# Output projection of a decoder block: seven products of halves for the first half of its inner dimension

## The chip, the cores and the metric

The kernel runs on one core of one Trainium2 chip. The metric is the time of one execution in device microseconds (us); lower is better. A core has five engines with a queue of instructions each: TensorE (PE in the profile; its weight loads are PEld), VectorE (DVE), ScalarE (ACT), GpSimd (POOL) and SyncE (SP), which here only issues DMA transfers. Each queue is worked off in its order, and an instruction that waits holds up those behind it.

## The reference, cut to what matters

One decoder block on 512 tokens with 1024 channels: two branches (stick-breaking attention, an RWKV-7 time mix) are merged by gates, projected and added to the residual, then come a squared-ReLU MLP and gated per-layer embeddings. The change lies in the line with `w_out`, a product of 512 x 1024 by 1024 x 1024.

```python
    g_sb, g_rw = jnp.split(jax.nn.sigmoid(u_gate), 2, axis=-1)
    merged = g_sb * (o_sb @ w_up_sb[i]) + g_rw * (o_rw @ w_up_rw[i])
    x = x + merged @ w_out[i]
    h = rms_norm(x, mlp_norm_g[i])
    x = x + jnp.square(jax.nn.relu(h @ w_ff1[i])) @ w_ff2[i]
```

## The kernel before, in words

All matrix products of this part are made in three passes: each operand x is kept as a rounded part hi and a rest lo = x - hi, and a product is hi*hi + hi*lo + lo*hi. For a weight tile, ScalarE writes hi (`fetch_to`, L220) and VectorE writes lo (L221); for an operand `split` does the same (L266, L267). So a weight unit of 128 x 1024 numbers (512 KB) costs a DMA load (L178, into one of four buffers `w_raw`), an ACT cast and a DVE subtraction. The hi and lo tiles rotate through three buffers, except for units with a home of their own (`homes`).

The order of the weight units is written out by hand in the list `seq`. `weights` takes the next unit; three steps of matmuls later (`step`, L241 on) the two units behind it are cast and one more is loaded. The framework then orders each engine's queue by its own estimate of when instructions become ready, in which what stands earlier in the program goes first among the ready ones. So loads run ahead of their place in the program as far as buffers are free, and a queue's order on the chip may be one that its times do not suit.

The stage of the change runs as follows (L1117 on). First the residual input x (`xs`, four loads, L1122) and the embedding input (`praw`, L1124) are asked for. Then eight steps m = 0 to 7 make the merged activations: two tiles `ga` and `gb` are loaded (L1130, L1131), ScalarE applies a sigmoid to `gb` (L1133), TensorE makes the product of the RWKV branch for 128 channels (12 matmuls, lines 236 to 238), VectorE multiplies (L1141), adds (L1142), and `split` writes hi and lo into `mg` (128 channels x 512 tokens each; m is the index k of the inner dimension). Then comes the output projection, in `rows3` (lines 251 to 253): six matmuls of 512 columns multiply one group of 128 tokens (tt, four of them) with one weight unit. A unit of `w_out` holds 256 rows of the inner dimension (two k) by 512 columns; units 0 to 3 are the left half of the columns, 4 to 7 the right half. `by_token` makes the left half for all four groups of tokens, unit by unit. The right half is made group by group with all four units. `taken` (L1153, L1155) adds a result to `xs` and sums its squares; `scaled` (L1165 to L1169) makes the norm of a group of tokens once both halves are in. After the third group, `gained` transposes the first two groups into `hx` (L1092, L1096, L1097), the input of the MLP. Results take turns in the eight PSUM banks (`ps_main`: two of pool `psm`, six of pool `ps4`).

The MLP behind it already makes its second product of each quarter by seven products of halves. There the sums of weight blocks are made by DMAs that add onto a tile already in memory, issued on POOL's queue: in `early_sums` (L1338 to L1341) one tile is loaded and a block added onto it, and that tile is then added onto a second one; a third such place is L180.

## Time and profile before

| | us |
|---|---|
| median of 3 runs | 859.14 (859.08 to 859.78) |
| the profiled execution, its time | 859.45 |
| its span in the profile | 857.6 |
| PE busy in the span | 842.7 |
| DVE busy | 696.3 |
| ACT busy | 502.3 |
| POOL busy | 102.2 |

Busy time of PE is the time in which at least one matmul was under way; matmuls overlap, so the duration of one (389 ns for 512 columns) is more than the distance to the next. The other engines' instructions overlap only a little at their ends. A group's line gives its engine, its operation, the tile written and those read, the shapes, the count, the busy time and mean duration, and the idle time of the engine in front of it. A DMA's line in a queue is its issue; the time to landing is told apart.

### The profile page before, as it was taken

Reading aid. Unit: us, or ns where it says so; the run is one execution under the profiler, and the core shown is the slowest. Engines: PE = TensorE matmul, PEld = TensorE weight load, DVE = VectorE, ACT = ScalarE, POOL = GpSimd, SP = SyncE. Lnnn points to the kernel's source line nnn. Section 1 sums busy time; section 2 is a strip of 40 time slices with the busy share of each in tenths; the row PEclk is TensorE's granted clock in tenths of the full one; section 3 lists DMA queues with packets and bytes.
Section 4 is the critical chain, followed back from the end, with each engine's and each line's share of the span. In section 5 each row is a group of like instructions: output and inputs, shape, how many; then the busy total and the mean of one; then the engine's idle time right before and its main releaser. Section 6 shows DMA issues by size and latency. Waiting matters only on the chain.

```text
span 857.6 us, 14532 instructions
## 1 busy us (share of the span) xinstructions
PE 842.7 (98%) x5570; PEld 697.4 (81%) x5570; DVE 696.3 (81%) x1238; ACT 502.3 (59%) x785; POOL 102.2 (12%) x170
## 2 busy tenths in 40 slices
PE   9999999999999999999999999999999999999996
PEld 5778788877777777877888887899889989988885
DVE  7989987896987978867763489998789988997767
ACT  7788887744436253534554666467547844873843
POOL 1332431001202111020000101000110011010000
PEclk9999999999999999999999999999999999999998
DMA  8212212221121314428950766964875589284402
GB/s 321 99 51 64 84 62 86 75 99 51 63 88 37 109 66 136 162 86 275 328 183 25 212 205 152 246 192 134 210 223 150 149 226 260 83 225 136 173 24 99
DMA packets 39333, 121.08 MB, mean 141 GB/s; under 512 B 4448, under 2 KB 4448, under 8 KB 39264
## 3 DMA queue, kind: packets, MB, share of 16 engines
q1 hardware_dynamic: 34656, 103.37, 35.0%
q0 software_dynamic: 4608, 16.78, 11.0%
q8 instruction: 44, 0.72, 0.4%
q14 instruction: 25, 0.20, 0.1%
HBM read 105.46 MB, written 10.49 MB: 135 GB/s over the span
## 4 chain that ended last, share of the span: by engine, by line
PE 80%; DVE 13%; ACT 2%; DMA 2%; issue 2%; SPq 0%; DVEq 0%; ACTq 0%
PE ps_m L236 13%; PE ps_m L237 13%; PE ps_m L238 12%; PE ps_m L252 9%; PE ps_m L253 9%; PE ps_m L251 9%; DVE w_lo L221 2%; DMA w_raw<-in_wts_dram 2%; PE ps_g L862 1%; PE ps_o L542 1%; PE ps_s L990 1%; PE ps_z L550 1%; PE ps_g L952 1%; PE ps_c L981 1%; DVE LX L884 1%
## 5 line engine op out<-in xcount | busy, mean ns | idle before, releaser
L220 ACT CAST w_hi<-w_raw 128x1024 fp32r<-128x1024 f32 x123 | 129.0, 1050 | 133.0 <-PE ps_m L237 74.5
L221 DVE TENSOR_TENSOR w_lo<-w_raw,w_hi 128x1024 fp32r<-128x1024 f32 x123 | 150.3, 1224 | 32.0 <-ACT w_hi L220 31.5
L236 PE MATMUL ps_m<-h_hi,w_hi 128*128 128x512 f32 x320 | 130.2, 408 | 0.1
L238 PE MATMUL ps_m<-h_hi,w_lo 128*128 128x512 f32 x320 | 128.5, 402 | 0.0
L237 PE MATMUL ps_m<-h_lo,w_hi 128*128 128x512 f32 x320 | 128.1, 400 | 0.1
L238 PEld LDWEIGHTS ps_m<-h_hi,w_lo 128*128 128x128 f32 x320 | 60.2, 188 | 11.9
L236 PEld LDWEIGHTS ps_m<-h_hi,w_hi 128*128 128x128 f32 x320 | 60.6, 190 | 11.2 <-ACT h_hi L398 0.6
L237 PEld LDWEIGHTS ps_m<-h_lo,w_hi 128*128 128x128 f32 x320 | 60.4, 189 | 11.2 <-DVE h_lo L399 1.2
L237 PE MATMUL ps_m<-hx,w_hi 128*128 128x256 f32 (+1 forms) x212 | 68.6, 324 | 0.1
L236 PE MATMUL ps_m<-hx,w_hi 128*128 128x256 f32 (+1 forms) x212 | 68.6, 324 | 0.0
L238 PE MATMUL ps_m<-hx,w_lo 128*128 128x256 f32 (+1 forms) x212 | 68.5, 323 | 0.0
L252 PE MATMUL ps_m<-w_lo,fS 128*128 128x512 f32 x128 | 50.0, 391 | 0.6 <-DVE w_lo L221 0.6
L251 PE MATMUL ps_m<-w_hi,fS 128*128 128x512 f32 x128 | 49.8, 389 | 0.0
L236 PE MATMUL ps_m<-tb,w_hi 128*128 128x256 f32 x176 | 49.8, 283 | 0.0
L237 PE MATMUL ps_m<-tb,w_hi 128*128 128x256 f32 x176 | 49.8, 283 | 0.0
L238 PE MATMUL ps_m<-tb,w_lo 128*128 128x256 f32 x176 | 49.8, 283 | 0.0
L253 PE MATMUL ps_m<-w_hi,fS 128*128 128x512 f32 x128 | 49.8, 389 | 0.0
L237 PEld LDWEIGHTS ps_m<-hx,w_hi 128*128 128x128 f32 x212 | 40.4, 190 | 3.5 <-DVE hx L1097 0.4
L236 PEld LDWEIGHTS ps_m<-hx,w_hi 128*128 128x128 f32 x212 | 40.4, 190 | 3.4 <-ACT hx L1096 0.2
L238 PEld LDWEIGHTS ps_m<-hx,w_lo 128*128 128x128 f32 x212 | 40.3, 190 | 3.1
L251 PE MATMUL ps_m<-w_hi,fA 128*128 128x512 f32 x96 | 37.4, 389 | 0.0
L252 PE MATMUL ps_m<-w_lo,fA 128*128 128x512 f32 x96 | 37.4, 389 | 0.0
(410 smaller groups left out, 2107.4 us busy)
## 6 DMA issues: line engine op xcount, KB each, us to landing
w_raw<-in_wts_dram SPq DMA_DIRECT2D x130, 512.0 KB, 3.8
gates<-gg SPq DMA_DIRECT2D x16, 256.0 KB, 2.0
w_raw<-in_wts_dram POOLq DMA_DIRECT2D x8, 512.0 KB, 6.4
x_in<-in_xT_dram SPq DMA_DIRECT2D x8, 256.0 KB, 5.3
tmp<-gates SPq DMA_DIRECT2D x8, 256.0 KB, 3.2
upsb<-tmp SPq DMA_DIRECT2D x8, 256.0 KB, 3.9
ga<-upsb SPq DMA_DIRECT2D x8, 256.0 KB, 5.2
gb<-gates SPq DMA_DIRECT2D x8, 256.0 KB, 5.0
```

Of the source, the lines that this page charges most:

```text
L220: state["cast"] = act.copy(out=hi, in_=raw).ins
L221: dve.tensor_tensor(out=lo, in0=raw, in1=r32(hi), op=ALU.subtract)
L236: pe.matmul(ps, wh, xh[:, k, t], start=first, stop=False, skip_group_check=skip)
L237: pe.matmul(ps, wh, xl[:, k, t], start=False, stop=False, skip_group_check=skip)
L238: pe.matmul(ps, wl, xh[:, k, t], start=False, stop=last, skip_group_check=skip)
L251: pe.matmul(ps, xh[:, k + j], wh, start=first and j == 0, stop=False, skip_group_check=True)
L252: pe.matmul(ps, xh[:, k + j], wl, start=False, stop=False, skip_group_check=True)
L253: pe.matmul(ps, xl[:, k + j], wh, start=False, stop=last and j == 1, skip_group_check=True)
L542: pe.matmul(ps_o[:, j * P:T], vv[:, j, hh, :, :].rearrange("p a d -> p (a d)"), part[:, ZB[j]:ZB[j] + ZN[j]], start=j == 2 and part is wh, ...
L550: pe.matmul(zt[b][:, :n], tri, part[:, s:s + n], start=False, stop=False, skip_group_check=True)
L862: last = pe.matmul(ps[rows, k], left[rows, k, :], rhs[rows, k], start=True, stop=True)
L884: beside = dve.transpose(out=N[rows], in_=LM[rows, :, r // 2, r % 2 * 32:r % 2 * 32 + 32])
```

## The change

The four blocks of `w_out` that belong to the first half of the inner dimension (units 0, 1, 4, 5, called B11, B21, B12, B22) and the four blocks of the merged activations that meet them (A11, A12, A21, A22: tokens 0 to 255 or 256 to 511, by k = 0, 1 or k = 2, 3) are multiplied by seven products of blocks in place of eight (Strassen's scheme in Winograd's form). A product is two groups of tokens times one weight unit.

- `sums_by_dma`: three new tiles are loaded and summed by DMA: T3 = B12 + B22, T2 = B11 + T3, T4 = B21 + T2. Loads on SP's queue, additions on POOL's. A further sum, B11 + B12 for product 3, is made in a buffer `w_raw` by a load and an addition.
- `left_sums` and `lefts`: four sums of blocks of the activations, made by VectorE for k = 0, 2 (after m = 2) and k = 1, 3 (after m = 3), split into hi and lo, and kept in `hx`, which is free until then. The block A21 is not needed in itself, so for m = 0 and 1 only 256 tokens are split.
- `by_halves`: the products in the order 0, 3, 2, 1, 4, 5, 6 (the list `ORDER`), on eight PSUM banks: V, W, `seeded` and `rest`, two each. Product 0 goes to V, and ScalarE copies V to `seeded`; 3 goes to W, 2 is accumulated on V; ScalarE copies W and V aside; 1 is accumulated on `seeded`, 4 on V; VectorE subtracts what was set aside from W; 5 is accumulated on W; VectorE writes `rest`; 6 is accumulated on V. The weights are B11 for product 0, B21 for 1, T2 for 2, B11 + B12 for 3, T3 for 4, B22 for 5 and T4 for 6.
- The second half of the inner dimension (units 2, 3, 6, 7) is accumulated on the eight banks group by group, left and right half of the columns in turn; units 2, 3 and 6 have homes.
- `xs` and `praw` are asked for after the loop over m, `praw` is split after the seven products, `ga` and `gb` of more steps lie in buffers that are free early, and `sqx` has one buffer in place of two.

```diff
@@ -52,6 +52,8 @@
 SEVEN = {(1, kp) for kp in range(3)} | {(q, kp) for q in (2, 3) for kp in range(4)}
 EARLY = (0, 2)
 FF2_FROM = {0: 0, 1: 2, 3: 0, 5: 6}
+ORDER = (0, 3, 2, 1, 4, 5, 6)
+FROM = {0: 0, 1: 1, 3: 0, 5: 5}
 
 
 K_ID, K_ONE, K_STRICT, K_INCL, K_B8, K_O8, K_S8, K_BO8, K_BO, K_TRI, K_NEG, K_CAUS = range(12)
@@ -144,7 +146,7 @@
             [(U_GRW, m) for m in range(4, 8)] + [(U_UPSB, m) for m in range(4)]]
     seq += mixes(0) + sum(FILL, [])
     seq += [(U_UPRW, m) for m in range(4)]
-    seq += [(U_OUT, m) for m in range(8)]
+    seq += [(U_OUT, "s", i) for i in ORDER] + [(U_OUT, m) for m in (2, 3, 6, 7)]
     seq += [(U_PLE, 0)]
     for qd in range(4):
         for kp in range(4):
@@ -167,6 +169,8 @@
             return wts[UBASE[U_FF2] + seq[i][1] * 8 + FF2_FROM[seq[i][2]] + seq[i][3]]
         if seq[i][0] == U_S12:
             return wts[UBASE[U_FF1] + seq[i][1] * 8 + seq[i][2] + 4]
+        if seq[i][1] == "s":
+            return wts[UBASE[seq[i][0]] + FROM[seq[i][2]]]
         return wts[UBASE[seq[i][0]] + seq[i][1]]
 
     def load_to(n):
@@ -178,6 +182,8 @@
                 sync.dma_start(out=loaded[i], in_=unit(i))
                 if seq[i][0] == U_FF2 and seq[i][2] == 3:
                     pool.dma_start(out=loaded[i], in_=wts[UBASE[U_FF2] + seq[i][1] * 8 + 4 + seq[i][3]], accum_op=ALU.add)
+                if seq[i][1:] == ("s", 3):
+                    pool.dma_start(out=loaded[i], in_=wts[UBASE[seq[i][0]] + 4], accum_op=ALU.add)
 
     def four_sums(i):
 
@@ -337,7 +343,7 @@
                     todo.remove(t)
 
 
-        t12 = pa.tile([P, T], F32, name="t12")
+        t12 = pa.tile([P, T], F32, name="t12", tag="t12")
         t13 = pa.tile([P, T], F32, name="t13")
 
         def mixed(i, dst):
@@ -1082,6 +1088,59 @@
                 rows3(pss[tt], w, rhs, tt, kk * 2, kk == 0, kk == 3)
         return pss
 
+    def sums_by_dma(u, tile_):
+
+        t2, t3, t4 = (tile_(n) for n in ("T2", "T3", "T4"))
+        for t, m in ((t3, 4), (t2, 0), (t4, 1)):
+            sync.dma_start(out=t, in_=wts[UBASE[u] + m])
+        pool.dma_start(out=t3, in_=wts[UBASE[u] + 5], accum_op=ALU.add)
+        for t, more_ in ((t2, t3), (t4, t2)):
+            pool.dma_start(out=t, in_=more_, accum_op=ALU.add)
+        for i, t in ((2, t2), (4, t3), (6, t4)):
+            sources[u, "s", i] = lambda t=t: t
+
+    def by_halves(u, left, V, W, seeded, rest, spare):
+
+        def run(i, pss, first):
+            w = weights(u, "s", i)
+            for t2 in range(2):
+                rows3(pss[t2], w, left[i], t2, 0, first, False)
+
+        def aside(pss):
+            got = [spare() for _ in range(2)]
+            for t, ps in zip(got, pss):
+                act.copy(out=t, in_=ps)
+            return got
+
+        run(0, V, True)
+        for t2 in range(2):
+            act.copy(out=seeded[t2], in_=V[t2])
+        run(3, W, True)
+        run(2, V, False)
+        third, second = aside(W), aside(V)
+        run(1, seeded, False)
+        run(4, V, False)
+        for t2 in range(2):
+            dve.tensor_tensor(out=W[t2], in0=W[t2], in1=second[t2], op=ALU.subtract)
+        run(5, W, False)
+        for t2 in range(2):
+            dve.tensor_tensor(out=rest[t2], in0=third[t2], in1=V[t2], op=ALU.subtract)
+        run(6, V, False)
+        return (seeded + V, W + rest)
+
+    def left_sums(S, kp, a, b, c, d):
+
+        sums = const.tile([P, 4, 256], F32, name="sums", tag="lora_w")
+        for out_, x, y, op in ((0, d, b, ALU.subtract), (1, c, d, ALU.subtract), (2, sums[:, 0], c, ALU.subtract), (3, a, sums[:, 2], ALU.add)):
+            dve.tensor_tensor(out=sums[:, out_], in0=x, in1=y, op=op)
+        split(S[0][:, kp * 4:kp * 4 + 4], S[1][:, kp * 4:kp * 4 + 4], sums)
+
+    def lefts(x, S):
+
+        A11, A12, A22 = ([t[:, k:k + 2, h * 256:h * 256 + 256] for t in x] for k, h in ((0, 0), (2, 0), (2, 1)))
+        S1, S3, S2, S4 = ([t[:, i::4] for t in S] for i in range(4))
+        return (A11, A12, S2, S1, S3, S4, A22)
+
     def gained(gname, half, src):
 
         for kp in range(KT // 2):
@@ -1118,15 +1177,14 @@
     with ExitStack() as s3:
         p3 = s3.enter_context(tc.tile_pool(name="p3", bufs=1))
         mg = [pa.tile([P, KT, T], F32R, name="mg0", tag="h_lo"), p3.tile([P, KT, T], F32R, name="mg1")]
-        for tt in range(TT):
-            sync.dma_start(out=xs[:, tt, :], in_=xt[:, tt, :])
-        praw = p3.tile([P, 2, T], F32, name="praw")
-        sync.dma_start(out=praw, in_=pT)
+        S = [t[:, 0:4].rearrange("p a (b t) -> p (a b) t", b=2) for t in hx]
+        sums_by_dma(U_OUT, lambda n: p3.tile([P, 1024], F32, name=n))
+        ups = []
         for m in range(8):
 
-            early = {0: ("mix", "mix"), 1: ("mix", "mix"), 2: ("gg", "gg")}.get(m)
-            ga, gb = (pa.tile([P, T], F32, name=n, tag=early[j], bufs=4 if early[j] == "mix" else 2) if early else
-                      p3.tile([P, T], F32, name=n, bufs=3) for j, n in enumerate(("ga", "gb")))
+            ga = pa.tile([P, T], F32, name="ga", tag="mix", bufs=4) if m < 4 else p3.tile([P, T], F32, name="ga", bufs=2)
+            gb = pa.tile([P, T], F32, name="gb", tag="t12" if m % 3 == 2 else "gg", bufs=1 if m % 3 == 2 else 2)
+            ups.append(ga)
             sync.dma_start(out=ga, in_=upsb[:, m, :])
             sync.dma_start(out=gb, in_=gates[:, KT + m, :])
             with tc.issue_after(state["norm"].ins):
@@ -1140,18 +1198,25 @@
             product(ps, w, orw, nk=4, base=m % 2 * 512)
             dve.tensor_tensor(out=gb, in0=ps, in1=gb, op=ALU.mult)
             dve.tensor_tensor(out=ga, in0=ga, in1=gb, op=ALU.add)
-            split(mg[0][:, m, :], mg[1][:, m, :], ga)
-        split(pin[0], pin[1], praw)
+            n = 256 if m < 2 else T
+            split(mg[0][:, m, 0:n], mg[1][:, m, 0:n], ga[:, 0:n])
+            if m in (2, 3):
+                x, y = ups[m - 2], ga
+                left_sums(S, m - 2, y[:, 0:256], y[:, 256:T], x[:, 0:256], x[:, 256:T])
+        for tt in range(TT):
+            sync.dma_start(out=xs[:, tt, :], in_=xt[:, tt, :])
+        praw = p3.tile([P, 2, T], F32, name="praw")
+        sync.dma_start(out=praw, in_=pT)
         wo = [[p3.tile([P, 1024], F32R, name=f"wo{kk}{i}") for i in range(2)] for kk in range(3)]
-        for kk in range(3):
-            homes[(U_OUT, 4 + kk)] = lambda kk=kk: wo[kk]
+        for kk, m in enumerate((2, 3, 6)):
+            homes[(U_OUT, m)] = lambda kk=kk: wo[kk]
         xsc = pa.tile([P, TT, D], F32, name="xsc", tag="h_hi")
 
         def taken(ps, tt, half):
 
             xb = xs[:, tt, COLHALF[half]]
             dve.tensor_tensor(out=xb, in0=ps, in1=xb, op=ALU.add)
-            sq = p3.tile([P, T], F32, name="sqx", bufs=2)
+            sq = p3.tile([P, T], F32, name="sqx")
             act.activation(out=sq, in_=xb, func=AF.Square, accum_out=st2[:, half, tt:tt + 1])
             if half == 0:
                 a, ah = st2[:, 0, tt:tt + 1], st2[:, 2, tt:tt + 1]
@@ -1167,16 +1232,16 @@
             dve.tensor_scalar(out=vh, in0=b, scalar1=-0.5 / D, scalar2=ah, op0=ALU.mult, op1=ALU.add)
             newton(r, n, vh, dve)
             state["scaled"] = act.activation(out=xsc[:, tt], in_=xs[:, tt], func=AF.Copy, scale=r).ins
-        pss = by_token(U_OUT, 0, mg, 0)
+        V, W, seeded, rest = ([ps_main() for _ in range(2)] for _ in range(4))
+        pss = by_halves(U_OUT, lefts(mg, S), V, W, seeded, rest, lambda: pa.tile([P, T], F32, name="aside", tag="mix", bufs=4))
+        split(pin[0], pin[1], praw)
+        ws = [weights(U_OUT, m) for m in (2, 3, 6, 7)]
+
         for tt in range(TT):
-            taken(pss[tt], tt, 0)
-        ws = [weights(U_OUT, 4 + kk) for kk in range(4)]
-
-        for tt in range(TT):
-            ps = ps_main()
-            for kk in range(4):
-                rows3(ps, ws[kk], mg, tt, kk * 2, kk == 0, kk == 3)
-            taken(ps, tt, 1)
+            for half in range(2):
+                for kk in range(2):
+                    rows3(pss[half][tt], ws[half * 2 + kk], mg, tt, 4 + kk * 2, False, kk == 1)
+                taken(pss[half][tt], tt, half)
             scaled(tt)
             if tt == 2:
                 gained("mlp_g", 0, xsc)
```

## The prediction

> **What bounds the kernel now.** I read the page first, then the waits of PE, then the timeline of the output projection.
>
> ```profile
> span 857.6 us, 14532 instructions
> PE   842.7 (98%) x5570; PEld 697.4 (81%) x5570; DVE 696.3 (81%) x1238; ACT 502.3 (59%) x785; POOL 102.2 (12%) x170
> L220 ACT CAST w_hi<-w_raw 128x1024 fp32r<-128x1024 f32 x123 | 129.0, 1050 | 133.0 <-PE ps_m L237 74.5
> ```
>
> PE is busy almost always. Its longest waits in the whole execution are small:
>
> ```profile
> PE ps_z L381 <- POOL warm L378: 1.3, 1, 1.3
> ...
> PE ps_m L252 <- DVE w_lo L221: 0.6, 2, 0.4
> ```
>
> In the stage of the change PE never stops, so here a matmul saved is time saved, and any wait put in front of one is time lost. The timeline of PE shows the first matmul of the projection (L251), the transposes within it and the first matmul behind it (`pins`):
>
> ```profile
> 424.80 0.39 PE L251 MATMUL ps_m<-w_hi,mg 128*128 128x512 f32 x1
> ...
> 462.89 1.91 PE L1092 MATMUL ps_m<-cst,xsc 128*128 128x128 f32 x16
> 464.55 0.48 PE L251 MATMUL ps_m<-wo,mg 128*128 128x512 f32 x1
> ...
> 470.10 0.39 PE L251 MATMUL ps_m<-w_hi,pins 128*128 128x512 f32 x1
> ```
>
> From 424.80 to 470.10 are 45.30 us; the transposes take 464.55 - 462.89 = 1.66. The other 43.64 hold 8 units x 4 groups x 6 = 192 matmuls, one per 0.227 us (the 0.39 of a row is its length; the next starts inside it).
>
> **Matmuls.** The first half of the inner dimension had 96 of them. Seven products of two groups x 6 = 12 make 84, and the second half keeps 96. So 12 go: 12 x 0.227 = 2.7 us, all on the path. This is also the ceiling, because PE had no wait here that could vanish. Each product now lasts 2.72 us where a unit lasted 5.45; the products start at 424.80, 427.5, 430.2, 433.0, 435.7, 438.4 and 441.1, the second half at 443.9.
>
> **VectorE.** Its groups from 402 to 445 us now:
>
> ```profile
> L221 DVE TENSOR_TENSOR w_lo<-w_raw,w_hi 128x1024 fp32r<-128x1024 f32 x8 | 9.8, 1220 | 5.4 <-ACT w_hi L220 5.4
> L1142 DVE TENSOR_TENSOR ga<-ga,gb 128x512 f32<-128x512 f32 x8 | 5.4, 686 | 0.1
> L267 DVE TENSOR_TENSOR mg<-ga,mg 128x512 fp32r<-128x512 f32 x8 | 5.4, 684 | 1.5 <-DMA upsb<-tmp 0.8 <-ACT mg L266 0.7
> L1141 DVE TENSOR_TENSOR gb<-ps_m,gb 128x512 f32<-128x512 f32 x8 | 5.4, 682 | 0.6 <-PE ps_m L238 0.6
> L221 DVE TENSOR_TENSOR wo<-w_raw,wo 128x1024 fp32r<-128x1024 f32 x3 | 3.6, 1212 | 0.0
> ...
> L267 DVE TENSOR_TENSOR pins<-praw,pins 128x1024 fp32r<-128x1024 f32 x1 | 1.2, 1225 | 2.9 <-ACT pins L266 2.9
> ```
>
> These are 30.8 us in 43. The added work has its like in the MLP, where the same sums and copies are made:
>
> ```profile
> L267 DVE TENSOR_TENSOR fS<-sums,fS 128x1024 fp32r<-128x1024 f32 x7 | 8.5, 1221 | 2.3 <-ACT fS L266 2.2
> L1217 DVE TENSOR_TENSOR sums<-sums,rr 128x256 f32<-128x256 f32 x7 | 3.0, 424 | 0.2
> ...
> L1191 ACT COPY rr<-ps_m 128x512 f32<-128x512 f32 x3 | 1.6, 595 | 0.0
> ...
> L1365 DVE TENSOR_TENSOR xs<-xs,ps_m x56: 678/680/684, 529.5 to 797.1; 128x512 f32<-128x512 f32 x56
> ```
>
> Three more weight units (11 for 8) are 3 x 1.22 = 3.7; `left_sums` 2 x (4 x 0.42 + 1.22) = 5.8; four subtractions from PSUM 4 x 0.68 = 2.7. Off go the split of `praw` (1.2, moved behind the products) and half of two `mg` splits (about 0.5). VectorE comes to about 41 us in 43, nearly full. What does a nearly full VectorE cost? Two stretches of the MLP bound it, beside the one that holds the loop over m:
>
> ```profile
> 405.20:430.00 24.80, 24.80 (x111) 20.53 (x110) 19.29 (x28) 13.29 (x19) 0.00 (x0) 1.00 0.89 315
> ...
> 530.00:545.00 15.00, 14.60 (x64) 11.75 (x63) 14.50 (x16) 6.56 (x7) 1.74 (x2) 1.00 0.97 240
> ...
> 575.00:590.00 15.00, 15.00 (x127) 15.00 (x127) 14.68 (x21) 12.04 (x19) 0.00 (x0) 1.00 0.35 121
> ```
>
> (Columns: length, then busy time of PE, PEld, DVE, ACT, POOL, clock, DMA share, GB/s.) At 14.50 of 15 PE lost 0.40, at 14.68 it lost nothing: 0 to 0.40 / 15 x 43 = 1.1 us. I take 0 for the load as such, since the fuller stretch lost nothing, and count the loss where a deadline is close (T2, below). Most of the added work has slack: the sums of the activations are wanted at 427.5, and `mg` of m = 4 to 7 only from 443.9 on.
>
> **ScalarE** gets three casts more (3 x 1.05), two for the sums (2 x 1.05) and six copies from PSUM (6 x 0.60), 8.9 us. It was busy 13.29 of 24.80, so there is room. The copies are each wanted a whole product later: V must be copied by 430.2 and was finished at 427.5. PE would lose what a copy came later than 2.7 us; I take 0.
>
> **The sums by DMA.** Seven transfers of 512 KB are added. Four of them are additions on POOL's queue, and two of these depend on each other ahead of product 2: T3 is loaded, B22 added onto it, then T3 onto T2. The tiles lie where the stage before lay; the first transfers that wait for that space now are those of `xs`:
>
> ```profile
> 401.79 0.33 SPq L178 DMA_DIRECT2D w_raw<-in_wts_dram  x1
> ...
> 408.13 1.76 SPq L1122 DMA_DIRECT2D xs<-in_xt_dram  x4
> ```
>
> So T3 is asked for at 408.13. The MLP's chain of the same kind gives its prices:
>
> ```profile
> L1338 SPq DMA_DIRECT2D B12a<-in_wts_dram x4: 328/328/328, 477.7 to 699.1; - x4
> ...
> DMA to landing us min/median/max: 3.4/4.3/6.3
> ```
>
> ```profile
> L1340 POOL DMA_DIRECT2D B12a<-in_wts_dram x4: 862/867/1033, 482.0 to 703.7; - x4
> ...
> DMA to landing us min/median/max: 5.6/7.6/10.2
> ```
>
> ```profile
> L1341 POOL DMA_DIRECT2D B11a<-B12a x4: 864/867/870, 490.1 to 718.1; - x4
> ...
> DMA to landing us min/median/max: 4.7/7.9/11.2
> ```
>
> ```profile
> 482.00 1.03 POOL L1340 DMA_DIRECT2D B12a<-in_wts_dram  x1 [103.86 <-DMA B11a<-in_wts_dram]
> ...
> 490.06 0.87 POOL L1341 DMA_DIRECT2D B11a<-B12a  x1 [4.59 <-DMA B12a<-in_wts_dram]
> ```
>
> The last two rows show one step of the chain with its hand-over: 8.1 us. By these rows T2 is there at 408.13 + 4.3 + 8.1 + 7.9 = 428.4. Its cast (1.05) and subtraction (1.22) end at 430.7. PE wants the subtraction's result for the second matmul of product 2, at 430.2 + 0.23 = 430.5: a wait of 0.2. Cast and subtraction also find engines at work; half an instruction of 0.68 us in front adds 0.3. I take 0.5 us. With the shortest landings (3.4 + 5.6 + 4.7) T2 is there at 421.8 and costs nothing; with the longest (6.3 + 10.2 + 11.2) at 435.8, and PE waits until 438.1, 7.6 us. T4 follows T2 by 7.9, at 436.3, and is wanted at 441.1; it is no later than T2 in its effect.
>
> The Trainium skill, page "DMA: Bandwidth & Descriptors", section "Anatomy of one DMA — SWDGE (gpsimd) path", has about 2.0 us and 436 GB/s for a DMA from this queue, by my estimate 3.2 us for 512 KB; by that T2 would be there at 418.8 and the sum the full 2.7. The rows above measured 7.6 and 7.9 for such additions, so they decide.
>
> **Moved loads.** `xs` is now asked for behind the loop's loads. `taken` wants it at 443.9 + 2.7 = 446.6, over 30 us after the space is free. Eight banks hold all results, so a late `xs` would reach PE only at the transposes behind group 3, some 14 us later. Nothing, unless SP's queue stands still that long. The transposes of `gained` meet a bank of V that group 4 still needs; 24 matmuls (5.4 us) can go ahead of them, so I take 0.
>
> **The sum.** -2.7 + 0.5 = -2.2 us. The profiled execution took 859.45, which gives 857.25; it lies 0.31 above the median of 859.14, so I forecast 856.9. About 0.2% (1.7 us) is what a measurement here can tell from no change.
>
> **Rivals.**
>
> *T2 is late.* For it: the loads around it. DMA was at its limit where the chain runs, as it was in the MLP where additions took their longest:
>
> ```profile
> 414.00:419.00 5.00, 5.00 (x24) 4.14 (x23) 1.87 (x2) 1.96 (x2) 0.00 (x0) 1.00 1.03 380
> ...
> 482.00:490.00 8.00, 8.00 (x37) 6.64 (x36) 2.83 (x3) 2.89 (x6) 1.90 (x2) 1.00 1.06 301
> ```
>
> Against it: here one chain runs, there two. If each addition takes 9 us, T2 comes at 430.4 and PE waits 2.2: -0.5, 858.6. Waits between 1.0 and 4.4 mean no visible change; that is a T2 between 429.2 and 432.6. With additions of 11 us (434.4) the wait is 6.2, +3.5, 862.6. The Trainium skill, same page, section "SWDGE vs HWDGE vs iDMA", says that the DMA engines take turns between the two kinds of queue; that the landings spread from 4.7 to 11.2 agrees.
>
> *VectorE's order.* In its queue the work on m = 6 and 7 (two times 0.68 x 3) may stand ahead of T2's subtraction while `gb` of m = 7 is still on its way. Two instructions back to back take less than their two durations:
>
> ```profile
> 426.33 1.28 DVE L267 TENSOR_TENSOR mg<-ga,mg 128x512 fp32r<-128x512 f32 x2
> ```
>
> (0.09 us less than twice 0.684.) From 403 to the end of T2's subtraction stand six weight units (6 x 1.22 = 7.3), eight times multiply and add (8 x 1.37 = 11.0), their splits (6 x 0.68 + 2 x 0.42 = 4.9) and `left_sums` (5.8), 29.0 by durations, some 26 with about 38 instructions back to back, for the 27.5 us up to 430.5. Each idle us above 1.5 is a wait: 1 to 3 us are likely in this case, so -1.7 to +0.3, about 858.4. Against it: the loads of `ga` and `gb` no longer queue behind `xs`.
>
> *POOL's order, slower.* Product 3 needs its own addition (B11 + B12), and all four stand in one queue:
>
> ```profile
> w_raw<-in_wts_dram SPq DMA_DIRECT2D x130, 512.0 KB, 3.8
> ...
> w_raw<-in_wts_dram POOLq DMA_DIRECT2D x8, 512.0 KB, 6.4
> ```
>
> The unit in its place was asked for at 401.79, so it could be there at 405.6 and be summed at 412.0, ahead of T3. But if that addition stands behind T4's, which waits for T2 until 428.4, it lands at about 428.4 + 0.9 + 6.4 = 435.7; with cast and subtraction 438.0 against 427.7: 10.3 us lost, +7.6, 866.7. It decides from the point where T4's addition is the earlier one in the queue. The early load speaks against it.
>
> **Chances.** Forecast (T2's wait under 1 us, no other) 0.47. T2 late without visible change 0.22, T2 so late that it is slower 0.09. VectorE's order 0.12, without visible change. POOL's order 0.10, slower. Faster 0.47, same 0.34, slower 0.19. The range goes from the full 2.7 with a little scatter, 856.0, to the part of the late T2 that is slower, 861.5. Since signs are mixed, the likeliest case's own range is 856.2 to 857.7.
>
> **What would show it.** PE: 180 matmuls at L251 to L253 in the projection, still 0.227 us apart; the `pins` matmuls at about 467.9 in place of 470.10. A wait of PE for `w_lo` or `w_hi` at product 2, near 430.5, shorter than 1 us, with T2's second addition landing near 428.4. DVE near 95% from 405 to 440. The forecast is wrong if T2 lands after 429, if a wait stands at product 3, or if POOL's additions come in another order.

## The result and the profile after

The changed kernel takes 865.98 us (865.38 to 866.82, 5 runs) where the kernel before, on the same chip, takes 859.08 (858.86 to 859.78, 5 runs): a ratio of 1.008 (95% interval 1.0066 to 1.0095), 6.9 us slower. The forecast was 856.9, 2.2 us faster. The mechanism that was to bring the gain is there; the time was lost beside it. Of all executions told of below one, of run 1, took 2112.6 us, with matmuls of 0.83 us all through; it is left out of the ratios.

The head of the page of the changed kernel, then PE's waits in the stage of the change (us in total, times, longest):

```profile
span 864.1 us, 14565 instructions
...
PE 843.2 (98%) x5558; PEld 695.8 (81%) x5558; DVE 707.3 (82%) x1255; ACT 509.4 (59%) x796; POOL 105.8 (12%) x174
```

```profile
PE ps_m L257 <- ACT ps_m L1117: 2.7, 1, 2.7
PE ps_m L258 <- DVE w_lo L227: 2.3, 1, 2.3
```

Before, PE had no wait in this stage. The 12 matmuls are gone (5558 for 5570). Line numbers behind the new functions are higher now: L257 to L259 are the three matmuls of `rows3`, L226 and L227 cast and subtraction of a weight unit, L1117 the copies V to `seeded`, L186 product 3's addition, L1095 to L1098 the loads and additions of T3, T2 and T4. The timeline of PE has both waits and both ends of the stage:

```profile
426.24 0.39 PE L257 MATMUL ps_m<-w_hi,mg 128*128 128x512 f32 x1
...
428.96 0.39 PE L257 MATMUL ps_m<-w_hi,hx 128*128 128x512 f32 x1
431.62 0.50 PE L258 MATMUL ps_m<-w_lo,hx 128*128 128x512 f32 x1 [2.27 <-DVE w_lo L227]
...
434.04 0.39 PE L259 MATMUL ps_m<-w_hi,hx 128*128 128x512 f32 x1
437.10 0.80 PE L257 MATMUL ps_m<-w_hi,hx 128*128 128x512 f32 x1 [2.67 <-ACT ps_m L1117]
437.69 0.78 PE L258 MATMUL ps_m<-w_lo,hx 128*128 128x512 f32 x1
...
440.33 0.40 PE L258 MATMUL ps_m<-w_lo,hx 128*128 128x512 f32 x1
...
476.17 0.39 PE L257 MATMUL ps_m<-w_hi,pins 128*128 128x512 f32 x1
```

From 426.24 to 476.17 are 49.93 us, for 45.30 before. Read from start to start, with the usual 0.227 taken off, the wait at product 3 costs 431.62 - 428.96 - 0.23 = 2.43 and the one at product 2 costs 437.10 - 434.04 - 0.23 = 2.83. Behind the second, seven matmuls take 440.33 - 437.10 = 3.23 us where 1.59 is usual: 1.64 more. That is 6.9; with -2.72 for the matmuls it makes 4.2 of the 4.63 that were lost. The stage is not all: the span is 6.5 us longer, and 1.44 of these lie ahead of the stage and 0.4 behind it. Of the 1.44, 1.2 are there some 120 us before the stage, in a place that the change does not touch (a matmul after a wait starts at 305.64 for 304.42); what makes them is open. The windows show why the seven were slow (columns as in the prediction; the clock is the last but two):

```profile
434.00:437.00 3.00, 0.43 (x2) 0.00 (x0) 1.81 (x3) 2.97 (x5) 0.64 (x1) 0.97 1.04 421
437.00:440.00 3.00, 2.90 (x7) 2.13 (x8) 2.52 (x4) 3.00 (x6) 0.00 (x0) 0.50 1.06 303
```

The granted clock fell to a half while PE stood still and came back 3 us after it ran again.

The wait at product 3 has its own chain. ScalarE stood for the gates of m = 5 and 6 (the loads `gb`), VectorE for ScalarE's casts behind them, and product 3's subtraction, whose w_hi was there at 425.0, stood in VectorE's queue behind the split of m = 5:

```profile
422.90 0.63 ACT L1191 ACTIVATE gb<-gb 128x512 f32<-128x512 f32 x1 [1.83 <-DMA gb<-gates]
...
428.56 0.63 ACT L1191 ACTIVATE gb<-gb 128x512 f32<-128x512 f32 x1 [1.24 <-DMA gb<-gates]
```

```profile
424.08 0.69 DVE L273 TENSOR_TENSOR mg<-ga,mg 128x512 fp32r<-128x512 f32 x1 [1.95 <-ACT mg L272]
...
429.74 0.69 DVE L273 TENSOR_TENSOR mg<-ga,mg 128x512 fp32r<-128x512 f32 x1 [0.75 <-ACT mg L272]
430.34 1.22 DVE L227 TENSOR_TENSOR w_lo<-w_raw,w_hi 128x1024 fp32r<-128x1024 f32 x1
...
436.40 1.22 DVE L227 TENSOR_TENSOR w_lo<-T,w_hi 128x1024 fp32r<-128x1024 f32 x1
```

The chain of waits tells who made PE stand still until 437.10 (start, length, what; "issue" here is T3's addition on its way, for which the profile has no row):

```profile
408.62 7.18 DMA T<-in_wts_dram
415.79 0.41 DVE sums L1135
416.21 0.38 issue
416.59 0.38 POOL T L1096
416.96 8.90 issue
425.86 0.01 POOLq L1098
425.88 7.61 DMA T<-T
...
433.59 1.05 ACT w_hi L226
434.64 0.53 ACT gb L1191
435.18 1.28 ACT L1194
436.47 0.58 ACT ps_m L1117
437.10 0.80 PE ps_m L257
```

This is the chain of the prediction up to T2's landing, 433.5 where 428.4 was forecast. Then it goes another way: ScalarE works off its queue in order, and in it T2's cast, the sigmoid of m = 7 and the table load (L1194) stand ahead of the copies V to `seeded`, which product 2 needs as it overwrites V. Its own row shows that it stood idle for T2:

```profile
433.59 1.05 ACT L226 CAST w_hi<-T 128x1024 fp32r<-128x1024 f32 x1 [3.88 <-DMA T<-T]
```

So the copies, whose operand V was there at 429.1, waited for T2's transfer. They are not the only thing that did: T2's own subtraction (the last row above) ended at 437.62, and the second matmul of product 2, which reads it, started at 437.69. With the copies in time PE would have stopped one matmul later, until about the same moment.

The DMA engines carry the difference. The stretch from 405 to 440 us, of the kernel before and then of the changed one, and the changed one's queues (packets, MB, share of 16 engines):

```profile
405.00:440.00 35.00, 35.00 (x157) 28.96 (x156) 27.09 (x35) 18.71 (x24) 0.00 (x0) 1.00 0.84 294
```

```profile
405.00:440.00 35.00, 30.06 (x126) 23.95 (x125) 26.35 (x40) 17.47 (x25) 3.64 (x4) 0.95 1.00 326
```

```profile
q1 hardware_dynamic: 3387, 9.44, 70.0%
q0 software_dynamic: 520, 1.93, 29.5%
```

They were busy 0.84 of the stretch and are busy all of it now. By the time of their packets the additions' 1.93 MB (q0) took 0.295 x 35 = 10.3 us of all 16 engines, the 9.44 MB of loads and stores 24.5 us: 5.3 us per MB against 2.6, so that an addition of 512 KB holds the engines 2.8 us and a load of that size 1.4. VectorE was busy 26.35 of 35 us, 75% and not 95%: it was not full, it stood and waited.

### The profile page after: what moved, and what is told of

Read it like the earlier page. It is cut to its first block, busy times and chain, and to the rows that moved or that the text cites. A ratio compares the mean times of both kernels' runs of the same rounds, so it can differ in the third digit from the quotient of the medians.

```text
span 864.1 us, 14565 instructions
## 1 busy us (share of the span) xinstructions
PE 843.2 (98%) x5558; PEld 695.8 (81%) x5558; DVE 707.3 (82%) x1255; ACT 509.4 (59%) x796; POOL 105.8 (12%) x174
## 4 chain that ended last, share of the span: by engine, by line
PE 77%; DVE 13%; DMA 4%; issue 3%; ACT 3%; SPq 0%; POOL 0%; ACTq 0%; DVEq 0%; POOLq 0%
PE ps_m L242 12%; PE ps_m L243 12%; PE ps_m L244 12%; PE ps_m L258 9%; PE ps_m L257 9%; PE ps_m L259 9%; DVE w_lo L227 2%; PE ps_g L868 1%; PE ps_o L548 1%; DMA T<-T 1%; DMA ple_d<-rr 1%; PE ps_s L996 1%; PE ps_z L556 1%; PE ps_g L958 1%; PE ps_c L987 1%
## 5 line engine op out<-in xcount | busy, mean ns | idle before, releaser
L226 ACT CAST w_hi<-w_raw 128x1024 fp32r<-128x1024 f32 x123 | 129.0, 1050 | 128.1 <-PE ps_m L243 71.6
L227 DVE TENSOR_TENSOR w_lo<-w_raw,w_hi 128x1024 fp32r<-128x1024 f32 x123 | 150.3, 1224 | 27.5 <-ACT w_hi L226 27.0
L257 PE MATMUL ps_m<-w_hi,fS 128*128 128x512 f32 x128 | 49.8, 389 | 0.0
L259 PE MATMUL ps_m<-w_hi,fS 128*128 128x512 f32 x128 | 49.8, 389 | 0.0
L259 PE MATMUL ps_m<-w_hi,fA 128*128 128x512 f32 x96 | 37.4, 390 | 0.0
```

Of the source, the lines that this page charges most:

```text
L226: state["cast"] = act.copy(out=hi, in_=raw).ins
L227: dve.tensor_tensor(out=lo, in0=raw, in1=r32(hi), op=ALU.subtract)
L257: pe.matmul(ps, xh[:, k + j], wh, start=first and j == 0, stop=False, skip_group_check=True)
L259: pe.matmul(ps, xl[:, k + j], wh, start=False, stop=last and j == 1, skip_group_check=True)
```

## Experiments

The stage is the time from the first matmul of the projection to the first on `pins`, in the profiled execution (45.30 before, 49.93 changed); the ratio is to the kernel before on the same chip. The order of instructions within an engine's queue is set by the planner, so that an edit in one place can move others. One such move matters in runs 2, 3, 4, 9 and 12: there a matmul of product 2, which overwrites V, stands directly behind product 0's twelve and ahead of product 3, so that PE wants the copies V to `seeded` 2.7 us earlier than in the changed kernel. In run 17 it stands behind the first matmul of product 3. The times of these runs do not measure their edit alone. The profiled executions of runs 5, 9 and 14 lie 2.9, 1.5 and 3.0 us above the median, so that their stage and waits are somewhat too long. Runs 1, 2, 3, 12 and 16 leave sums out and compute something else.

| kernel | us | ratio (95%) | stage | waits of PE in it |
|---|---|---|---|---|
| no additions (1; 16) | 860.1; 857.93 | 1.001 (1.0001 to 1.002) | 43.79 | 0.5 |
| no left sums (2) | 870.4 | 1.0132 (1.0115 to 1.0148) | 56.68 | 11.2 |
| neither (3) | 862.48 | 1.0042 (1.0028 to 1.0056) | 46.95 | 1.7, 0.4 |
| `xs` late (4) | 868.13 | 1.0093 (1.0065 to 1.0121) | 50.97 | 5.5 |
| copies first (5) | 864.83 | 1.0052 (1.0033 to 1.0071) | 50.15 | 4.2, 0.6 |
| order (6) | 863.69 | 1.0048 (1.0032 to 1.0064) | 48.64 | 3.0, 1.5 |
| sums on GpSimd (7) | 866.56 | 1.0075 (1.0058 to 1.0091) | 51.29 | 6.1 |
| order, GpSimd (8) | 866.7 | 1.0077 (1.0061 to 1.0092) | 51.06 | 5.0, 0.7 |
| gates first (9) | 869.17 | 1.0106 (1.0078 to 1.0135) | 54.18 | 8.5 |
| new order (10) | 871.84 | 1.0137 (1.0112 to 1.0163) | 55.42 | 4.0, 3.2, 1.7 |
| new order, gates first (11) | 872.24 | 1.0142 (1.0112 to 1.0171) | 57.01 | 5.7, 4.7 |
| plain operands (12) | 865.69 | 1.0066 (1.0041 to 1.009) | 50.57 | 4.7 |
| prompt copies (13) | 868.87 | 1.0112 (1.0097 to 1.0127) | 54.34 | 8.3 |
| and m = 6, 7 late (14) | 866.88 | 1.0082 (1.0056 to 1.0108) | 53.77 | 4.0, 2.0, 1.2 |
| and left sums late (15) | 867.34 | 1.0095 (1.007 to 1.0121) | 51.62 | 3.6, 0.8, 0.4 |
| sums on VectorE (17) | 863.54 | 1.0053 (1.0037 to 1.007) | 48.16 | 2.9 |
| before, with transfers (18) | 861.01 | 1.0014 (1.0005 to 1.0024) | 45.30 | none |

### One part left out

**1, no additions.**

```
-        pool.dma_start(out=t3, in_=wts[UBASE[u] + 5], accum_op=ALU.add)
-        for t, more_ in ((t2, t3), (t4, t2)):
-            pool.dma_start(out=t, in_=more_, accum_op=ALU.add)
```

> The three additions by DMA onto T2, T3 and T4 are left out (the tiles hold the plain blocks of weights); the order of the instructions on PE, DVE, ACT and SP is that of the changed kernel. Theory (late T2): product 2 waited because T2 was complete only at 433.5 us and ScalarE, which works in order, stood at T2's cast from 429.7 to 433.6, with the copies of V to the banks called seeded behind it. Without the additions PE's second wait (2.7 us) and the stretch of half clock behind it (about 1.7 us) go, and the wait at product 3 (2.3 us) stays: about 861.6. Rival (VectorE and ScalarE are simply too full): the casts and copies come no earlier, at most 0.5 us is won: about 865.5.

860.1: 5.9 us came back, so with the three additions most of the loss goes. But the gain of 2.7 did not come. Run 16 is the same kernel in one profiled execution, 857.93; it is read below.

**2, no left sums.** The calls of `left_sums` go, and `lefts` returns plain quarters.

```
-        return (A11, A12, S2, S1, S3, S4, A22)
+        return (A11, A12, A11, A12, A22, A12, A22)
```

> The four sums of blocks of the activations are left out (plain blocks stand in their places): VectorE loses 5.8 us of work and ScalarE 2.1 us; the matmuls stay. Theory (late T2): the wait at product 3 goes, but product 2 still waits for T2 until about 434, so PE's second wait grows by what the first loses: about 865 to 866. Rival (VectorE too full): both waits shrink, 862 or less.

Both theories missed: 870.4, with one wait of 11.2 us for the copies. T3's addition went out at 418.1 in place of 416.6, T2 landed at 438.0 after 10.6 us on its way, and the copies came behind its cast. A T2 that is 4.5 us later, and an order on PE that wants the copies 2.7 us earlier, together cost 4.4 us more; what less work for VectorE is worth, the run does not tell.

**3, neither.** Both edits.

> Both are left out: no additions by DMA, no sums of activations. What is left is the plan of the matmuls with its loads, casts and copies. If the matmul term of 2.7 us is right and only those two costs stood against it, this is at about 856.4 with no wait of PE in the stage. If the copies from PSUM or the three additional weight units cost time by themselves, PE waits here too and it stays above 857.5.

862.48, slower than without the additions alone by 2.4. The trace shows why. With product 2 directly behind product 0 the copies are wanted at 428.5; the first of them stood behind the table load and T2's cast in ScalarE's queue and ended at 430.3. PE waited 1.7 for it and then 0.4 for T2's w_lo, and the clock was at half behind that.

**4, `xs` late.** The loads of `xs` and `praw` wait until the weights of unit 3 of the second half are asked for.

```
+        with tc.issue_after(state["late"]):
             for tt in range(TT):
                 sync.dma_start(out=xs[:, tt, :], in_=xt[:, tt, :])
```

> The loads of xs and praw (2.5 MB) are issued only behind the load of unit 3, after the chain of additions; everything is computed. Theory (late T2 through crowded DMA): loads of T tiles and additions land faster (5 to 7 us in place of 7.2 to 9.0), T2 is there by about 429 and the time falls to 861 to 863. Rival (an addition takes its time whatever else is loaded): T2 stays near 433 and the time near 866.

868.13. T2's own addition took 5 us and not 7.6, but T3's took 9 as before, T2 landed at 432.5, and PE waited 5.5 for the copies. So the early loads of `xs` are not what makes T2 late: without them it comes 1.0 us sooner. The time itself tells less, as PE's order is another one.

### T2 earlier, or wanted later

**5, copies first.** The fetch that casts T2 is issued behind the copies.

```
+            state["due"] = state["due"] if i else 0
...
+        got = state["seed"] = [act.copy(out=seeded[t2], in_=V[t2]) for t2 in range(2)][1]
+        with tc.issue_after(got.ins): fetch_to(state["used"] + AHEAD - 1, 1)
```

> T2's cast, and with it the next ones, is put behind the two copies V to seeded in ScalarE's queue; nothing else is changed on purpose (the split of praw goes behind them too). Theory A (T2 lands late by its two additions, and ScalarE's queue then makes the copies wait for it): the copies end near 431 and PE's 2.7 us wait becomes a shorter one, for T2 itself, which landed at 433.5 in the changed kernel: about 864.0, 2 us under the changed kernel. Theory B (ScalarE and VectorE have too much work in the stage, whatever its order): 865.5 to 867.

864.83, near theory A's 864.0, though not by the way it gave. In the profiled execution (867.77) the wait for the copies is gone; in its place PE waits 2.3 for product 3's w_lo, and 0.6 and 1.9 for T2's cast and w_lo. In this kernel's chain stand two loads of `gb`, 6.8 and 7.7 us long, with VectorE behind them: T2 is not the only operand that is late.

**6, order.** Products 0, 3, 1, 2, 5, 4, 6.

```
-ORDER = (0, 3, 2, 1, 4, 5, 6)
+ORDER = (0, 3, 1, 2, 5, 4, 6)
...
+        third = aside(W)
+        run(1, seeded, False)
+        run(2, V, False)
+        second = aside(V)
+        run(5, W, False)
```

> The same seven products in the order 0, 3, 1, 2, 5, 4, 6 in place of 0, 3, 2, 1, 4, 5, 6, with the copies and subtractions moved with them; all the results are the same sums. T2 is wanted 2.7 us later, and the copies V to seeded no longer stand behind its cast. Theory A: the 2.7 us wait and the slow clock behind it go, and a wait of at most 1.5 for T2 comes; the wait of 2.3 at product 3 stays: about 862.5. Theory B: 865 to 867.

863.69: 2.3 us back. No wait for the copies; the w_lo of product 3 (2.6) stays, and product 6 now waits 1.5 for the subtraction that reads V.

**7, sums on GpSimd.**

```
+        b22 = pool_.tile([P, 1024], F32, name="b22", tag="praw"); sync.dma_start(out=b22, in_=wts[UBASE[u] + 5])
+        for t, more_ in ((t3, b22), (t2, t3), (t4, t2)):
+            pool.tensor_tensor(out=t, in0=t, in1=more_, op=ALU.add)
```

> The three additions of T3, T2 and T4 are made by GpSimd's own tensor_tensor on loaded tiles (B22 gets a load and the space of praw) in place of DMA additions. GpSimd's 128x256 addition took 0.80 us, so a 128x1024 one is some 3.2 and T2 is there before 424. Theory A: no wait for T2, none for the copies; what stays is the wait of up to 2.3 at product 3: 858 to 860. Theory B (the engines' load, and GpSimd beside VectorE on top): 865 or more.

Theory A fails: T2 was ready near 425.5 and the time is 866.56. PE waits 6.1 us for product 3's w_lo. GpSimd's rows, and VectorE's beside them (L1200 adds two tiles in SBUF and takes 0.69 elsewhere, L1135 0.42; L1199 reads one operand from PSUM):

```profile
420.38 2.39 POOL L1098 TENSOR_TENSOR T<-T,b 128x1024 f32<-128x1024 f32 x1 [10.77 <-DMA ga<-upsb]
422.85 5.28 POOL L1098 TENSOR_TENSOR T<-T,T 128x1024 f32<-128x1024 f32 x2
```

```profile
422.98 2.88 DVE L1200 TENSOR_TENSOR ga<-ga,gb 128x512 f32<-128x512 f32 x1
425.78 0.68 DVE L1199 TENSOR_TENSOR gb<-ps_m,gb 128x512 f32<-128x512 f32 x1
426.38 2.02 DVE L1135 TENSOR_TENSOR sums<-ga 128x256 f32<-128x256 f32 x1
```

While GpSimd adds, VectorE's additions of two SBUF tiles take 2.88 and 2.02 us; the one with a PSUM operand keeps its 0.68. The Trainium skill, "SBUF — State Buffer", section "Who interferes with whom", says that a VectorE instruction with two inputs in SBUF contends with a GpSimd instruction that reads SBUF; the rows agree.

**8, both.** Edits of 6 and 7.

> Both together: GpSimd's additions and the order 0, 3, 1, 2, 5, 4, 6. Theory A: the time of the additions on GpSimd alone, within 0.6 us, as the order has nothing left to hide. Theory B: 865 or more.

866.7, as 7 alone: the wait for the w_lo of product 3 (5.0) stands ahead of all that the order can help.

### Order of loads, and of the queues

**9, gates first.** The call of `sums_by_dma` goes behind the loads of m = 3.

```
+            if m == 3:
+                with tc.issue_after(got.ins): sums_by_dma(U_OUT, lambda n: p3.tile([P, 1024], F32, name=n))
```

> The loads of T3, T2 and T4 are issued behind the loads of ga and gb of m = 3, in place of ahead of them. Theory D (the added transfers fill the DMA engines from 410 to 440, so the loads of ga and gb land late, VectorE stands still for them, and product 3's w_lo stands behind that in its queue): VectorE's idle time near 421 to 424 goes and the 2.3 us wait at product 3 falls under 1; T2 lands 2 to 3 us later, and the wait at product 2 grows by as much: 865 to 868. Theory V (VectorE and ScalarE have too much work, the order of the loads is nothing): both waits stay as they are, 866.

869.17, above both theories. T2 lands at 436.3, 2.8 later, as theory D had it, and PE waits 8.5 for the copies behind its cast. That no wait shows at product 3 is no proof of theory D: the first matmul of product 2 now stands ahead of product 3, and product 3's w_lo, there at 431.2, would still have come 1.6 after the 429.6 at which the old order wants it.

**10, new order**, 1, 5, 0, 3, 2, 4, and 6 behind the first two groups of the second half.

```
+ORDER = (1, 5, 0, 3, 2, 4, 6)
...
+        run(1, seeded, True)
+        run(5, W, True)
+        fifth = aside(W)
         run(0, V, True)
+        zeroth = aside(V)
+        for t2 in range(2): dve.tensor_tensor(out=seeded[t2], in0=seeded[t2], in1=zeroth[t2], op=ALU.add)
+        run(3, W, False)
```

> The products in the order 1, 5, 0, 3, 2, 4 and 6 behind the second half of the first two groups, with copies and subtractions arranged for it (the same sums; two subtractions and two additions on VectorE more, two copies PSUM to PSUM less). T2 is wanted 6.8 us later than in the changed kernel, T4 later still. Theory D: the waits for T2 and for the copies go; the second product still waits up to 2.3 us for its w_lo, which stands at the same place in VectorE's queue: about 861.5. Theory V: the additional VectorE work makes it 866 or more.

**11, with gates first** (edit of 9).

> Both together: the new order of the products, and the loads of T3, T2 and T4 behind those of m = 3. Theory D: neither wait is left, or under 1 us: 857 to 860. Theory V: 866 or more.

871.84 and 872.24. T2 is wanted 6.8 us later and no longer matters, but PE now waits 4.0 and 4.7 for the new additions on VectorE (L1120) and 3.2 and 5.7 for the cast of a weight unit, for whose load ScalarE had stood 3.9 and 6.4 us. The order that gives T2 more time brings new turns from PE to VectorE and back, and PE waited at them.

**12, plain operands.** `FROM` gets entries for products 2, 4 and 6, and `sums_by_dma` is not called.

```
+FROM = {0: 0, 1: 1, 2: 0, 3: 0, 4: 4, 5: 5, 6: 1}
```

> The sums T3, T2 and T4 are left out with their preloaded tiles: products 2, 4 and 6 take plain blocks, loaded just in time as ordinary weight units (so the output is another). The 7 units with their casts and subtractions, the sums of the activations, all copies and product 3's addition stay; bytes are those of the kernel without additions, and nothing stands ahead of the loads of ga and gb. Theory D: no wait over 1 us, 856.5 to 858. Theory V: 860 or more, as without the additions alone.

Theory D, as it was put here, fails: 865.69 without a single sum of weights but product 3's. The same stretch as above, and the end of product 0 on PE:

```profile
405.00:440.00 35.00, 30.26 (x122) 24.43 (x121) 26.71 (x39) 18.03 (x25) 1.04 (x1) 0.90 0.79 257
```

```profile
428.15 0.39 PE L259 MATMUL ps_m<-w_hi,mg 128*128 128x512 f32 x1
433.28 1.22 PE L257 MATMUL ps_m<-w_hi,hx 128*128 128x512 f32 x2 [4.74 <-ACT ps_m L1117]
```

The DMA engines were busy 0.79 of the stretch, less than before the change. ScalarE's queue had the sigmoid of m = 7, the table load, product 2's cast and a cast of `mg` ahead of the copies, which ended at 433.7; PE waited 4.7 for them, directly behind product 0. Product 2's cast waited for no load: it began at 431.18, as the table load ended. So the loss came back without the three additions and without full DMA engines, by what stood where in the queues of ScalarE and PE.

**13, prompt copies.** Products 0, 1, 3, 5, 2, 4 and late 6; each set of copies ahead of the next fetch.

```
+ORDER = (0, 1, 3, 5, 2, 4, 6)
...
+        def then(copies):
+            state["copied"] = copies[-1].ins
+            with tc.issue_after(state["copied"]): fetch_to(state["used"] + AHEAD - 1, 1)
```

> The products in the order 0, 1, 3, 5, 2, 4 and 6 behind the second half of the first two groups (the same sums, no VectorE work added); T2's cast, the casts behind it and the split of praw are put behind the copies that PE waits for. The sigmoids of m = 6 and 7 and the table load still stand ahead of the copies V to seeded. Theory Q (what costs time is the order inside the queues of ScalarE and VectorE: copies and subtractions that PE wants within a product, 2.7 us, stand behind work on m = 3 to 7 that waits for its loads): T2's wait goes, but the copies come near 432 where 429 is wanted and the second product's w_lo near 431: one wait of 3 to 4 us and half a clock behind it, 862 to 865. Theory D (the DMA engines are full, so the operands are late in any order): 864 or more here and in the next two.

**14, and m = 6, 7 late.** Their sigmoids, `mult`, `add` and split, and the table load, are issued in `joins`, behind the copies V to `seeded`.

```
+        def joins(copy):
+            with tc.issue_after(copy.ins):
+                for m, ps, ga, gb in late:
+                    last = act.activation(out=gb, in_=gb, func=AF.Sigmoid)
+                    joined(m, ps, ga, gb)
```

> The same, and the sigmoids, sums and splits of m = 6 and 7 and the table load are put behind the copies V to seeded (they are wanted only for the second half). Theory Q: the copies come near 430; what is left is the second product's w_lo, a wait of up to 2.3: 859 to 862. Theory D: 864 or more.

**15, and left sums late.** The second call of `left_sums` goes behind the second product's subtraction, its split into `joins`.

> The same, and the sums of the activations of m = 2 and 3 are put behind the second product's subtraction on VectorE, and their split behind the copies. Theory Q: no wait over 1 us is left, 856.5 to 859. Theory D: 864 or more.

Theory Q fails as the whole cause: 868.87, 866.88, 867.34. Step by step the waits that it names shrink (8.3 for the copies, then 4.0, then 0.8; the w_lo to 0.4), and as each goes another comes. In 15 it is a plain weight unit, product 5's, 2.68 us late, and PE waits 3.6 for the copies behind its cast:

```profile
438.77 1.04 ACT L226 CAST w_hi<-w_raw 128x1024 fp32r<-128x1024 f32 x1 [2.68 <-DMA w_raw<-in_wts_dram]
```

### What the additions cost, and why

**16, no additions again**, one execution with a profile (edit of 1).

> The kernel without the three additions of T3, T2 and T4 (left out, as before), for a profile. Theory Q: the copies V to seeded still stand behind two sigmoids, the table load and T2's cast, so PE waits 1 to 3 us at the copies, and up to 2 for the w_lo of product 3: the 3 to 4 us by which this kernel misses the gain. Theory D: neither wait is there, and the time is lost in front of the stage.

Its only wait in the stage, its busy times and queues from 405 to 440, the copies in ScalarE's timeline, and T2's subtraction in VectorE's:

```profile
PE ps_m L258 <- DVE w_lo L227: 0.5, 1, 0.5
```

```profile
405.00:440.00 35.00, 34.53 (x151) 28.02 (x151) 31.74 (x46) 24.09 (x34) 1.04 (x1) 1.00 0.85 292
```

```profile
q1 hardware_dynamic: 3431, 9.66, 75.7%
q0 software_dynamic: 144, 0.52, 9.2%
```

```profile
427.17 0.62 ACT L1191 ACTIVATE gb<-gb 128x512 f32<-128x512 f32 x1
427.81 1.28 ACT L1194 ACT_TABLE_LOAD   x1
429.10 1.06 ACT L1117 COPY ps_m<-ps_m 128x512 f32<-128x512 f32 x2
```

```profile
430.23 1.23 DVE L227 TENSOR_TENSOR w_lo<-T,w_hi 128x1024 fp32r<-128x1024 f32 x1
```

The stage takes 43.79, 1.51 less than before and 6.1 less than with the additions. ScalarE's order is that of the changed kernel, and PE's products stand in the same order, with the same work ahead of the copies; they end at 430.2, and product 2 begins at 431.2. The margin that the prediction put at a whole product is 1.0 us even here, and T2's w_lo has none: its subtraction ends at 431.46, and the matmul that reads it starts at 431.51, where 431.43 was due. VectorE is busy 31.74 of 35 us, more than in the changed kernel (26.35), and PE lost next to nothing: a VectorE without room is not what cost the time. The one addition left (product 3's) held the DMA engines 0.092 x 35 = 3.2 us. That the nine timed executions of run 1 lie between 859.2 and 861.5 fits so thin a margin; that is an inference, as there is no trace of them.

**17, sums on VectorE.** As 7, with `dve` for `pool`.

```
+            dve.tensor_tensor(out=t, in0=t, in1=more_, op=ALU.add)
```

> The three additions of T3, T2 and T4 are made by VectorE (1.22 us each) on loaded tiles, in place of DMA additions; products and copies as in the changed kernel, and so are the sums. Theory D (the DMA additions hold the DMA engines about 2.8 us each where a load of the same size holds them 1.3, so everything behind them lands late): T2 is there before 424, the DMA engines are as in the kernel without additions, and 3.7 us more of VectorE stand partly in its idle time near 416 to 421: 859.5 to 862. Theory V (VectorE has no room): 864 or more, PE waiting for w_lo.

863.54, between the two theories: 2.4 us back. VectorE stood 2.16 us for the load of B22, added at 419.95, 422.23 and 423.97, and put all behind it later; the split of the second left sums ended at 432.5. PE waits once, 2.9 us, put down to the copies; product 3's w_lo ended at 433.65, so that PE would have stood until then without them.

**18, the kernel before with the transfers.**

```
+        for t, m in zip(extra, (0, 4, 1)):
+            sync.dma_start(out=t, in_=wts[UBASE[U_OUT] + m])
+        for t, more_ in ((2, wts[UBASE[U_OUT] + 4]), (1, wts[UBASE[U_OUT] + 5]), (0, extra[1]), (2, extra[0])):
+            pool.dma_start(out=extra[t], in_=more_, accum_op=ALU.add)
```

> The kernel before, with the three loads and four additions of 512 KB that the change brings (into tiles that nothing reads, at the same place in the queues) and its buffers and its place for the loads of xs; eight units as before, no product of halves. Theory D1 (the transfers alone delay the stage): 862 or more, with PE waiting for mg or for weights. Theory D2 (the transfers delay the operands, but only products of 2.7 us with copies and operands between them can't bear it; the units of 5.45 us can): 858.5 to 860.5, with the loads of ga and gb as late as in the changed kernel.

```profile
405.00:440.00 35.00, 35.00 (x156) 28.97 (x156) 22.04 (x30) 14.76 (x20) 3.67 (x4) 1.00 1.00 320
```

The DMA engines are as full as in the changed kernel (1.00), VectorE and ScalarE got 5 and 4 us less done in the stretch than before, `w_raw` loads took 9.9 us (median) where they took 4.2, and PE did not stop once: the stage is 45.30 us, what it was. D2 holds. The 1.4 us of this kernel lie outside the stage, 0.87 ahead of it and 1.0 behind.

**What follows.** It is shown that the transfers alone, with the changed buffers of `ga` and `gb`, cost the old stage nothing (18), that the short products in the same order of queues but without the three additions run almost without a wait (16, one execution), and that both together lose 6 us. So neither the traffic nor the products lose the time by themselves: full DMA engines make T2, the gates and the weights late, and products of 2.7 us with copies between them have no slack for that. The additions are not the only way to use that slack up: in 12, without them and with the DMA engines less full, what stood ahead of the copies in the queues lost as much. Which operand is late first depends on the order, and no order tried was free of it. Making the same sums elsewhere (7, 17) made VectorE late. No version with the reference's results was faster than the kernel before. How the loss splits among T2, the gates and the weights was not separated. Open stay also the 0.2 to 3.1 us that these kernels lose ahead of the stage (18 has 0.87 of it with the products unchanged, 5 has 3.1).

## Why the prediction was wrong, point by point

**Matmuls, right.** 12 fewer, 0.227 us apart where the clock is whole; without the additions 1.51 of the 2.7 appears, and 0.5 more but for a wait (run 16, one execution). In the nine comparable executions of run 1 no gain showed.

**The sums by DMA: the step that failed.** "By these rows T2 is there at 428.4." It was there at 433.5. T3 was asked for 0.5 later than the row said, its load took 7.2 where the MLP's median of 4.3 was taken, 0.8 passed until its addition went out, and the addition with its hand-over took 9.3 for 8.1; only the last, 7.6, was as priced. The prices came from a stretch with its own traffic. What was missing was a sum over the DMA engines: 0.84 busy before leaves 0.16 x 35 = 5.6 us, and the change asked for four additions at 2.8 and three loads at 1.4, 15 us. The prediction had the row with a share of 1.03 and used it for a rival only.

**ScalarE: the other step that failed.** "The copies are each wanted a whole product later ...; I take 0." The room was counted in time and not in queue order. Up to four instructions stood ahead of the copies, one of them waiting for T2. With T2 at 433.5 the prediction's own rule gives PE a wait until 436.1; it was 437.1 through the copies, and T2's subtraction would have held PE until 437.6 without them. The half clock, which no term had, added 1.6.

**VectorE.** The load as such cost nothing, as taken (run 16: 91% busy, 0.5 us of wait); but the 95% were 75%, because it waited. The rival *VectorE's order* came true in two places. At T2's subtraction, where it was expected, work on m = 7 stood ahead: the subtraction ended 3.0 us after the cast where it takes 1.22. And it hit product 3's, 2.4 us, which the prediction had as a sign against itself and priced at nothing.

**T2 is late**, the rival that came true, was priced at 858.6 for additions of 9 us. With T2 at the measured 433.5 its rule gives a wait of 5.6 and 862.0: still too low, as it left out the wait at product 3, the queue behind the cast, the half clock and what was lost ahead of the stage.

**POOL's order** did not come: product 3's addition went out first, at 407.8. **Moved loads**: `xs` went out at 415.8, not behind the loop's loads, and cost no wait of its own; asking for it late moved T2 by 1.0 us (4). The transposes cost about 0.2 us more than before.

**The range** ended at 861.5, though the bound of T2's chain was 435.8 and its wait 7.6, which makes 864.0: the bound was worked out and not used.

## What to carry to other kernels

Where transfers are added to a stretch, sum their time on the DMA engines against what is free there, additions at twice a load, before pricing any landing. Where a change puts a turn (PE to another engine and back) into a stage, write down what stands ahead of that step in the other engine's queue and what each of those waits for: the slack is what that queue leaves, not the time to the next use. And a saving that shortens every step also shortens every deadline; operands that were just in time for the long steps can be late for the short ones (18 against the changed kernel).

## What the runs showed of the hardware

A DMA addition of 512 KB held the DMA engines 2.8 us by the time of its packets (1.93 MB in 10.3 us; 3.2 in run 16), a load 1.4.

A wait of PE can cost more than its length. After 2.27 us the clock was whole; after 2.67 us it was 0.50 for 3 us, which cost 1.64. The length of the wait does not decide it alone: after 2.62 us in run 6 the clock was whole, and in run 14 it was whole still at the first matmul behind a wait of 3.96, fell 0.6 us later and stayed at half for 6.8. In run 2, with a wait of 11.2 us, it fell about 2.2 us after PE's last matmul ended and came back about 4.6 after the next began:

```profile
428.00:431.00 3.00, 0.47 (x3) 0.05 (x1) 2.36 (x5) 2.21 (x4) 0.24 (x1) 0.94 0.95 283
431.00:434.00 3.00, 0.00 (x0) 0.00 (x0) 1.70 (x3) 1.46 (x2) 0.00 (x0) 0.50 0.97 251
...
440.00:443.00 3.00, 3.00 (x7) 2.05 (x7) 3.00 (x4) 2.59 (x4) 0.00 (x0) 0.50 1.07 292
443.00:446.00 3.00, 3.00 (x11) 2.40 (x11) 0.93 (x2) 0.59 (x1) 0.00 (x0) 0.78 0.64 193
```

The Trainium skill, "TensorE: Matmul & The Clock Gate", section "What's actually happening", has half clock after an idle window of about 3.4 us and full clock after a busy one as long. The half agrees, and the way back (3.1 and 4.6 us of work) lies about its figure; the fall came sooner in these two, 2.4 and 2.2 us after the last matmul, and later in run 14, 4.5.

GpSimd's `tensor_tensor` stretched VectorE's additions of two SBUF tiles from 0.69 to 2.88 and from 0.42 to 2.02 us (run 7).
